# A spread of recurrence units, three operations on another engine, and seven early maps in a one-layer trunk kernel

## The chip, the cores and the metric

The kernel runs on one core of a Trainium2 chip. The metric is the device time of one execution in microseconds (us); lower is better. A core has TensorE (PE; its weight loads are shown apart as PEld), VectorE (DVE), ScalarE (ACT), GpSimd (POOL) and SyncE (SP), each with its own queue of instructions that it takes in order, and 16 DMA engines. Matrix results land in banks of PSUM, all else lies in SBUF or in DRAM.

## What is computed

The reference is one layer of a trunk for 512 latent tokens and 256 context tokens with a width of 1024. Cut to what matters here:

```python
p_l = modulate(x, norm1_g[l], mod[:, 0], mod[:, 1]) @ w_in[l]
pool_l, q_l, k_l, v_l, rw_l, gate_l = split_cols(p_l, IN_SPLITS)
att_l = diff_post(diff_attn_latent(qh_l, keys, vals, lam), subln_g[l], lam_init)
prep_c = rwkv_prepare(rw_c, *rw_par)
S_c, y_c = wkv_bidir(S0, *prep_c[:6])
prep_l = rwkv_prepare(rw_l, *rw_par)
_, y_l = wkv_bidir(S_c, *prep_l[:6])
rwo_l = rwkv_output(y_l, prep_l, r_k[l], gn_w[l], gn_b[l])
mix_l = merge_branches((pool_mixer(...), att_l, rwo_l), gate_l, w_br[l], w_out[l])
x = x + mod[:, 2] * mix_l
x = x + mod[:, 5] * hier_moe(f_l, *moe_par).reshape(B, L, D)
```

Three branches are merged: a pooling over windows of tokens, differential attention, and a recurrence that runs in both directions (`wkv_bidir`; each step updates a 64x64 state per head with a decay, a rank-one correction and a new key and value). A mixture of 32 experts follows.

## The kernel before

The recurrence is computed in chunks of 64 tokens. A unit is one of three groups of 256 tokens, one of two directions and one pair of heads (`g`, `d`, `hp`): 24 units. For each, `prep` makes the decays from a small matmul (L514, L515 into the banks `psm`): tanh on ScalarE (L518, L519), an affine step to a sigmoid (L520), a running sum `cum` (L522), exponentials of it (L524, L526) and, of the decays, the column `wc` at the end of each chunk (L527). From these come the scaled rows `abd`, `rbd` and `bk` (L531 to L540, of which L538 is an affine step on `ta`), and then products and transposes on TensorE (L552 to L584), masked by VectorE (L565, L587, L589) and copied by ScalarE (L571 to L591) into `ub`, which is stored in DRAM as `u_d`. After the eighth unit of a group `solve` loads small triangular blocks `pa_` of all eight from `u_d` and inverts them on VectorE, 30 steps of a product and an addition in sequence (L614, L616), and stores `t_d`.

`finish` makes of each unit its maps: it loads `tbd` from `t_d` and `ar` and `F` from `u_d`, and runs four steps of matmuls, L799, L805, L812 and then L831 (first group) or L824 (others), with copies on ScalarE between them (L800, L807), and additions on VectorE (L817, L833, L827). There are five `tbd` buffers. `steps` then runs the recurrence over the maps (L857).

The work is staged like this. First come the projections of the recurrence's inputs. Then the blocks for keys, queries and values (L231, token-major), pools and gates (L217, channel-major), each matmul three times with high and low parts of weights that ScalarE and GpSimd split (L211, L212); a pool block ends in a small matmul L684 into `psm`. A loop over these blocks starts one `prep` whenever enough steps have passed: `PACE = 34` spreads the 24 units over 34 of 52 steps. What is running lies in the list `active`, and each step of the loop (`tick`) advances each of its generators to its next `yield`. The last three gate blocks are `rest`. Then `NP = 4` turns of `finish` are begun before the pools of the first part are closed; the rest of the loop (`for i in range(NP, 24 + lag)`) begins a unit in each turn and advances attention by two pieces, and the recurrence by one step, once its maps are there. The scores of attention (L992, L993) go into one buffer `sc`; their softmax is L994 to L1004, the transposes are L1019, the weighted sums L1025, and the norm of a head ends in L1038. `bonus` makes a further term of the output (L904 to L919). The merges of the three branches (L1127), the output projection (L1418), the router and the experts (L1580, L1615, with weights loaded at L1231) follow.

The framework orders the instructions of each engine ahead of the run, by the order in which they are written and by priorities; `tc.high_priority(n)` moves what is written under it forward. Each engine's order is then fixed.

## Time and profile before

| | us |
|---|---|
| median of 3 runs | 1483.42 (1483.1 to 1486.53) |
| the profiled execution | 1484.0 |
| its span, first to last instruction | 1482.2 |
| PE busy | 1362.9 (92%) |
| DVE busy | 828.9 (56%) |
| ACT busy | 461.1 (31%) |
| POOL busy | 382.9 (26%) |

The shares are means over stages with different limits; what a stage waits for is read from stretches of the span. The mean granted clock of TensorE was 0.967. Idle time of an engine that does not set the pace costs nothing.

### The profile page before, as it was taken

Reading aid. Unit: us, or ns where it says so; the run is one execution under the profiler, and the core shown is the slowest. Engines: PE = TensorE matmul, PEld = TensorE weight load, DVE = VectorE, ACT = ScalarE, POOL = GpSimd, SP = SyncE. Lnnn points to the kernel's source line nnn. Section 1 sums busy time; section 2 is a strip of 40 time slices with the busy share of each in tenths; the row PEclk is TensorE's granted clock in tenths of the full one; section 3 lists DMA queues with packets and bytes.
Section 4 is the critical chain, followed back from the end, with each engine's and each line's share of the span. In section 5 each row is a group of like instructions: output and inputs, shape, how many; then the busy total and the mean of one; then the engine's idle time right before and its main releaser. Section 6 shows DMA issues by size and latency. Waiting matters only on the chain.

```text
span 1482.2 us, 23832 instructions
## 1 busy us (share of the span) xinstructions
PE 1362.9 (92%) x9076; PEld 1015.1 (68%) x9076; DVE 828.9 (56%) x1746; ACT 461.1 (31%) x1017; POOL 382.9 (26%) x345
## 2 busy tenths in 40 slices
PE   5999998898889898899999998995999999999987
PEld 3776787777779886788887776983555555445543
DVE  4553228789999765267777876452343343333324
ACT  4432244564545322234345423331110110111100
POOL 2111263354543343212221347110011111111101
PEclk9999999999899999799999999998999999999999
DMA  9368655565557673875747286479999999999996
GB/s 372 125 233 309 220 178 185 200 214 198 178 209 229 215 201 121 236 231 173 250 137 238 86 275 240 156 267 382 345 417 418 417 418 418 419 418 419 417 418 237
DMA packets 138615, 401.01 MB, mean 271 GB/s; under 512 B 38821, under 2 KB 69541, under 8 KB 107776
## 3 DMA queue, kind: packets, MB, share of 16 engines
q1 hardware_dynamic: 102640, 332.72, 61.0%
q10 hardware_dynamic: 32256, 58.47, 10.7%
q0 software_dynamic: 3600, 8.24, 1.7%
q8 instruction: 74, 1.21, 0.3%
q14 instruction: 45, 0.37, 0.1%
HBM read 344.47 MB, written 58.72 MB: 272 GB/s over the span
## 4 chain that ended last, share of the span: by engine, by line
PE 51%; DMA 27%; DVE 13%; issue 3%; ACT 2%; POOL 2%; SPq 1%; ACTq 0%; DVEq 0%; POOLq 0%
PE pp L217 11%; DMA ew<-in_w_eg_dram 8%; PE pp L1580 6%; DMA ew<-in_w_eu_dram 5%; DMA ew<-in_w_ed_dram 4%; PE pp L1127 4%; PE pp L1418 3%; PE pp L1615 3%; DVE ptmp L614 2%; PE pp L231 2%; PE pp L824 2%; PE sc L993 2%; PE pp L812 1%; PE pp L799 1%; PE pp L805 1%
## 5 line engine op out<-in xcount | busy, mean ns | idle before, releaser
L1580 PE MATMUL pp<-ew,xT 128*64 128x256 f32 x1888 | 225.4, 385 | 13.0 <-DMA ew<-in_w_eu_dram 7.1
L1580 PEld LDWEIGHTS pp<-ew,xT 128*64 128x64 f32 x1888 | 132.7, 137 | 93.5 <-issue 17.6
L217 PE MATMUL pp<-xll,wh 128*128 128x512 f32 x344 | 136.3, 397 | 0.9 <-DVE xll L317 0.7
L217 PE MATMUL pp<-xlh,wh 128*128 128x512 f32 x344 | 135.3, 404 | 1.3 <-DVE qn L666 1.0
L217 PE MATMUL pp<-xlh,wl 128*128 128x512 f32 x344 | 136.0, 396 | 0.0
L212 POOL TENSOR_TENSOR wl<-wraw,wh 128x512 fp32r<-128x512 f32 x84 | 115.1, 1399 | 75.4 <-ACT wh L211 71.7
L1633 POOL TENSOR_TENSOR yhl<-m,yhl 128x512 fp32r<-128x512 f32 x30 | 38.1, 1271 | 346.0 <-ACT yhl L1632 346.0
L1615 PE MATMUL pp<-ew,hT 128*64 128x512 f32 x440 | 101.4, 598 | 2.6 <-DMA ew<-in_w_ed_dram 2.6
L1586 DVE TENSOR_TENSOR hh<-hh,pp 128x256 f32<-128x256 f32 x32 | 13.5, 421 | 156.7 <-ACT hh L1585 156.7
L1618 DVE SCALAR_TENSOR_TENSOR m<-pp,gc,m 64x512 f32<-64x512 f32 x62 | 46.5, 750 | 85.1 <-PE pp L1615 73.3
L1625 DVE TENSOR_TENSOR x<-x,pp 128x512 f32<-128x512 f32 x128 | 79.8, 680 | 25.1 <-PE pp L1624 25.1
L211 ACT ACTIVATE wh<-wraw 128x512 fp32r<-128x512 f32 (+1 forms) x112 | 61.0, 614 | 61.8 <-PE pp L217 43.4
L217 PEld LDWEIGHTS pp<-xlh,wh 128*128 128x128 f32 x344 | 64.8, 190 | 19.3 <-issue 3.6
L217 PEld LDWEIGHTS pp<-xll,wh 128*128 128x128 f32 x344 | 65.2, 190 | 15.8 <-issue 1.8
L217 PEld LDWEIGHTS pp<-xlh,wl 128*128 128x128 f32 x344 | 65.2, 189 | 15.2 <-issue 1.1
L1615 PEld LDWEIGHTS pp<-ew,hT 128*64 128x64 f32 x440 | 29.4, 136 | 59.5 <-issue 48.2
L793 POOL TENSOR_TENSOR ao<-ar,cst 128x512 f32<-128x512 f32 x24 | 30.6, 1274 | 144.4 <-PE pp L805 81.8
L1594 ACT ACTIVATE hT<-psm 128x256 f32<-128x256 f32 x32 | 12.3, 384 | 157.4 <-PE psm L1592 129.7
L231 PE MATMUL pp<-wh,xlh 128*128 128x256 f32 x192 | 58.6, 305 | 0.0
L231 PE MATMUL pp<-wh,xll 128*128 128x256 f32 x192 | 56.8, 296 | 0.0
L231 PE MATMUL pp<-wl,xlh 128*128 128x256 f32 x192 | 56.6, 295 | 0.0
L1585 ACT ACTIVATE hh<-pp 128x256 f32<-128x256 f32 x32 | 12.3, 385 | 130.0 <-PE pp L1580 130.0
(407 smaller groups left out, 3112.0 us busy)
## 6 DMA issues: line engine op xcount, KB each, us to landing
ew<-in_w_eg_dram SPq DMA_DIRECT2D x59, 1024.0 KB
ew<-in_w_eu_dram SPq DMA_DIRECT2D x58, 1024.0 KB
ew<-in_w_ed_dram SPq DMA_DIRECT2D x56, 1024.0 KB
wraw<-in_w_in_dram SPq DMA_DIRECT2D x27, 1024.0 KB
u_d<-ub ACTq DMA_DIRECT2D x16, 1152.0 KB
wada<-in_w_adr_dram SPq DMA_DIRECT2D x16, 1024.0 KB
ar<-u_d SPq DMA_DIRECT2D x24, 640.0 KB
wa<-in_w_ad_dram SPq DMA_DIRECT2D x8, 1024.0 KB
```

What stands on the lines that cost most here:

```text
L211: S.activation(self.h[:, kk, :n], raw[:, kk, :n], AF.Copy)
L212: (eng[q % 2] if type(eng) is tuple else eng).tensor_sub(self.l[:, kk, :n], raw[:, kk, :n], self.h[:, kk, :n].bitcast(FT))
L217: PE.matmul(ps, a[:, k, cs], b[part][:, k], start=(k + n == 0), stop=(k == KD - 1 and n == 2))
L231: PE.matmul(ps, a[part][:, k, ts], b[:, k], start=(n == 0), stop=(n == 3 * KD - 1))
L793: G.tensor_mul(ao, aa[:, :, 2:3].to_broadcast([128, 4, 2, 64]), offm[:, None].to_broadcast([128, 4, 2, 64]))
L1127: PE.matmul(ps, a[:, k], bs[k][:, x], start=(c == 0), stop=(c == 11))
L1418: PE.matmul(p, a[:, ts], x[:, k], start=(k == 0 and c == 0), stop=(k == KD - 1 and c == 2))
L1580: PE.matmul(pg[64 * h:64 * h + 64, i], xT[:, k], of(w[i], k)[:, h * 256:h * 256 + 256], start=(k == 0), stop=(k == KD - 1), tile_position= ...
L1615: PE.matmul(pd[64 * h:64 * h + 64], hT[:, k], of(w[2], k)[:, h * 512:h * 512 + 512], start=(k == 0), stop=(k == 3), tile_position=(0, 64 * h))
L1618: V.scalar_tensor_tensor(y[ps_, h * 512:h * 512 + 512], pd[64 * h:64 * h + 64], gc, m5[ps_, h * 512:h * 512 + 512], op0=OP.mult, op1=OP.mult)
L1625: V.tensor_add(xt2[t][:, sl], xt2[t][:, sl], p)
L1633: eng.tensor_sub(yl, y[:, sl], yh.bitcast(FT))
```

## The change

`PACE` becomes 44, so the 24 units are spread over 44 of the 52 steps. Three operations per unit, L520, L527 and L538, become ACTIVATEs on ScalarE; the chunk ends `wc` are now exponentials of `cum` instead of copies of the decays. The blocks of `rest` are all written out before the first pools are closed, `NP` becomes 7, and the first seven turns of `finish`, and the memsets of their buffers, are written under a priority that moves them ahead, into the last projections. While these run, their matmuls use the two banks of `psm` instead of the six of `pp`, and the pools' last matmul L684 uses `pp` instead. The load of `pool_w` is written earlier into another pool, and `bonus` begins in a later turn.

```diff
--- before.py
+++ after.py
@@ -32,13 +32,13 @@
 GM = 6
 CL = 6
 AH = 5
-PACE = 34
+PACE = 44
 NF = 14
 NATT = 8
 PW = 4
 NG = 8
 NA = 4
-NP = 4
+NP = 7
 SW = 4
 FB = 2
 
@@ -346,6 +346,7 @@
     lpool = pa.enter_context(tc.tile_pool(name="lora", bufs=1, reuse_waits="tile"))
     wlT = lpool.tile([128, T], FT)
     alT = lpool.tile([128, T], FT)
+    pw = lpool.tile([128, 4, 128], FT)
 
     rw_ = pa.enter_context(ExitStack())
     rw = rw_.enter_context(tc.tile_pool(name="rwproj", bufs=1, reuse_waits="tile"))
@@ -517,14 +518,14 @@
         ta = wk.tile([128, 256], FT, name="ta", bufs=2)
         S.activation(sg, psw[:, 0:256], AF.Tanh, scale=0.5, bias=hb[:, dc:dc + 1])
         S.activation(ta, psw[:, 256:512], AF.Tanh, scale=0.5, bias=hb[:, 8 + dc:9 + dc])
-        V.tensor_scalar(sg, sg, 0.5, 0.5, op0=OP.mult, op1=OP.add)
+        S.activation(sg, sg, AF.Copy, scale=0.5, bias=0.5)
         cum = wk.tile([128, 256], FT, name="cum", bufs=1)
         V.tensor_tensor_scan(cum, K("scan"), sg, 0.0, OP.mult, OP.add)
         wt = wtb[u % NB]
         S.activation(wt[:, :, 1:65], c4(cum), AF.Exp, scale=DECAY)
         wi = wk.tile([128, 256], FT, name="wi", bufs=2)
         S.activation(wi, cum, AF.Exp, scale=-DECAY)
-        V.tensor_copy(wc[:, g, d, hp, :], wt[:, :, 64])
+        S.activation(wc[:, g, d, hp, :], c4(cum)[:, :, 63], AF.Exp, scale=DECAY)
         ab, rb = abd[u % NB], rbd[u % NB]
         for h in range(2):
             hs = slice(h * 64, h * 64 + 64)
@@ -535,7 +536,7 @@
         t1 = wk.tile([128, 256], FT, name="t1", bufs=1)
         V.scalar_tensor_tensor(t1, ta, 1.0, wi, op0=OP.add, op1=OP.mult)
         V.scalar_tensor_tensor(bk[:, :, 1], c4(t1), -0.5, c4(kk_), op0=OP.mult, op1=OP.mult)
-        V.tensor_scalar(ta, ta, ka[:, 0, hp:hp + 1], ka[:, 1, hp:hp + 1], op0=OP.mult, op1=OP.add)
+        S.activation(ta, ta, AF.Identity, scale=ka[:, 0, hp:hp + 1], bias=ka[:, 1, hp:hp + 1])
         V.tensor_mul(ta, ta, k_)
         V.tensor_mul(bk[:, :, 0], c4(ta), c4(wi))
         if lat:
@@ -619,14 +620,13 @@
         V.memset(pa_.rearrange("p i j -> p (i j)")[:, 0:1024:33], 1.0)
         nc.gpsimd.dma_start(t_d[g], pa_)
 
+    nc.sync.dma_start(pw, I["pool_w"])
 
     kp = pr_.enter_context(tc.tile_pool(name="qkv", bufs=1, reuse_waits="tile"))
     gq = kp.tile([128, 2, 64], FT)
     nc.sync.dma_start(gq, I["qkg"].partition_broadcast(128))
     tab = kp.tile([128, 4, 2, 64], FT)
     nc.sync.dma_start(tab, I["rope"])
-    pw = kp.tile([128, 4, 128], FT)
-    nc.sync.dma_start(pw, I["pool_w"])
 
     def qk_post(which, b, t, qn):
         yield 1
@@ -680,7 +680,7 @@
     def pool_post(g, u, cn):
         for _ in range(PW):
             yield 1
-        po = ps_sm()
+        po = ps_big()
         PE.matmul(po, pw[:, g], cn, start=True, stop=True)
         S.activation(u, po, AF.Copy, scale=P("ps", g))
         nc.scalar.dma_start(br_d[g], u)
@@ -728,6 +728,8 @@
             active.append(order.pop(0))
         next(rest, None)
         tick()
+    for _ in rest:
+        pass
     pr_.close()
     psol.close()
     dump("v_d", v_d)
@@ -758,12 +760,18 @@
     NT = 5
     tbd = [we.tile([128, 4, 128], FT, name=f"tbd{i}") for i in range(NT)]
     hbd = [we.tile([128, 4, 2, 2, 64], FT, name=f"hbd{i}") for i in range(2)]
-    for t_ in tbd + hbd:
-        V.memset(t_, 0.0)
+    with tc.high_priority(2000):
+        for t_ in tbd + hbd:
+            V.memset(t_, 0.0)
     units = {}
     cnt_f = [0]
 
+    early = [True]
+
     def ps2():
+
+        if early:
+            return ps_sm()
         return ppool.tile([128, 512], FT, name="pp", bufs=6)
 
     def finish(g, d, hp):
@@ -1068,11 +1076,10 @@
     lag = 6
     for i in range(NP):
         fin.append(finish(i // 8, i // 4 % 2, i % 4))
-        if i % 2:
-            next(rest, None)
-        turn(None, 0)
-    for _ in rest:
-        pass
+
+        with tc.high_priority(2000):
+            turn(None, 0)
+    early.clear()
     pa.close()
     psum = pb.enter_context(tc.tile_pool(name="psum2", space=PSUM, **TW))
     wk = pb.enter_context(tc.tile_pool(name="rwork", **TW))
@@ -1090,7 +1097,7 @@
             fin.append(finish(i // 8, i // 4 % 2, i % 4))
         g, j = divmod(i - 8 - lag, 8)
         turn(chains[g] if g >= 0 else None, 0 if i < NA else 2)
-        if 5 <= i < 13:
+        if NP < i < NP + 9:
             next(bon, None)
     wx.close()
     mgx = ctx.enter_context(ExitStack())
```

TensorE's order around the products of unit 24, before (line numbers are those of the file):

```order
L552 MATMUL psm<-cst,pr 128x2 x2
L563 MATMUL pp<-bk,abd_1700 128x128 x4
L569 MATMUL pp<-cst,bk 128x128 x4
L576 MATMUL pp<-cst,abd_1700 128x128 x4
L584 MATMUL pp<-rbd_1704,bk 128x128 x4
L231 MATMUL pp<-wh,xlh 128x256
L231 MATMUL pp<-wl,xlh 128x256
```

The same place after, where L553 to L585 are the lines L552 to L584 of before:

```order
L553 MATMUL psm<-cst,pr 128x2 x2
L564 MATMUL pp<-bk,abd_1701 128x128 x4
L570 MATMUL pp<-cst,bk 128x128 x4
L577 MATMUL pp<-cst,abd_1701 128x128 x4
L585 MATMUL pp<-rbd_1705,bk 128x128 x4
L217 MATMUL pp<-xlh,wh 128x512
L217 MATMUL pp<-xll,wh 128x512
```

Before, the last 120 matmuls of L231 (values) and 336 of L217 stand behind unit 24; after, no L231 and 216 of L217.

VectorE's order in the preparation of unit 24, before, where `pa__4521` and `ptmp` belong to the second `solve`:

```order
L520 TENSOR_SCALAR sg<-sg 128x256
L616 TENSOR_TENSOR pa__4521<-pa__4521,ptmp 128x30
L522 SCALAR_TENSOR_TENSOR cum<-cst,sg 128x256
L614 TENSOR_TENSOR ptmp<-pa__4521 128x29x2
L616 TENSOR_TENSOR pa__4521<-pa__4521,ptmp 128x29x2
L614 TENSOR_TENSOR ptmp<-pa__4521 128x28x3
L527 COPY wc<-wtb_1710 128x4
L531 TENSOR_TENSOR abd_1700<-lkk,wtb_1710 64x4x64 x2
```

And after, with lines that are one higher:

```order
L523 SCALAR_TENSOR_TENSOR cum<-cst,sg 128x256
L532 TENSOR_TENSOR abd_1701<-lkk,wtb_1711 64x4x64 x2
L537 SCALAR_TENSOR_TENSOR t_5088<-ta,wi 128x256
L538 SCALAR_TENSOR_TENSOR bk<-t_5088,lkk 128x4x64
L540 TENSOR_TENSOR ta<-ta,lk 128x256
L541 TENSOR_TENSOR bk<-ta,wi 128x4x64
```

The three operations are gone from VectorE's queue, and the second `solve` stands wholly ahead of this unit.

TensorE's order at the first maps, before, from the last projections to the first scores:

```order
L217 MATMUL pp<-xlh,wl 128x512
L799 MATMUL pp<-ar,tbd_5792 128x64 x4
L805 MATMUL pp<-z,ao 128x64 x4
L799 MATMUL pp<-ar,tbd_5793 128x64 x4
L812 MATMUL pp<-z_5844,tbd_5792 128x64 x4
L805 MATMUL pp<-z,ao 128x64 x4
L799 MATMUL pp<-ar,tbd_5794 128x64 x3
L992 MATMUL sc<-kh,qz 128x512
```

And after, where L807 is the first step of a map (L799 of before):

```order
L217 MATMUL pp<-xll,wh 128x512
L807 MATMUL psm<-ar,tbd_5792 128x64 x4
L217 MATMUL pp<-xlh,wl 128x512
L217 MATMUL pp<-xlh,wh 128x512
L217 MATMUL pp<-xll,wh 128x512
L217 MATMUL pp<-xlh,wl 128x512
L684 MATMUL pp<-wide,pw 128x512
```

The first map step now has 148 of the projections' matmuls behind it in TensorE's queue, and its result goes to a bank of `psm`; before, it stood behind the last projection. Up to the first score 6 groups of map matmuls stand before, and 21 after.

## Rows read from the trace of the kernel before

**Rows 1.** Stretches: length; busy time (instructions) of each engine; clock, DMA share, GB/s.
```profile
core 0: us, PE busy (x) PEld busy (x) DVE busy (x) ACT busy (x) POOL busy (x), PEclk, DMA share, GB/s
220.00:340.00 120.00, 107.92 (x713) 94.76 (x712) 98.21 (x242) 62.50 (x155) 51.48 (x49) 0.97 0.62 206
340.00:500.00 160.00, 139.48 (x881) 125.28 (x880) 154.03 (x356) 78.76 (x190) 66.60 (x63) 0.90 0.58 198
500.00:600.00 100.00, 93.05 (x443) 76.87 (x442) 53.48 (x107) 25.08 (x46) 38.13 (x32) 0.97 0.57 176
600.00:640.00 40.00, 34.19 (x180) 28.44 (x180) 15.79 (x35) 9.89 (x25) 9.16 (x12) 0.74 0.95 276
640.00:780.00 140.00, 140.00 (x1194) 121.15 (x1195) 97.01 (x185) 59.60 (x140) 32.60 (x34) 1.00 0.61 185
780.00:985.00 205.00, 193.44 (x1372) 164.05 (x1368) 144.56 (x310) 81.32 (x183) 70.55 (x54) 0.97 0.58 204
985.00:1482.00 497.00, 455.66 (x3093) 252.67 (x3092) 176.92 (x334) 66.20 (x132) 57.15 (x47) 0.98 0.97 393
```
**Rows 2.** Waits of SP's queue, 860 to 1000: total us, times, longest.
```profile
SPq L1231 <- PE pp L1418: 44.3, 4, 25.8
```
**Rows 3.** First unit's matmul (first and last start), unit 24's product and its mask.
```profile
L514 PE MATMUL psm<-wlT,w2p x48: 376/480/792, 218.5 to 462.7; 64*128 64x256 f32 x48
...
492.15 2.08 PE L563 MATMUL pp<-bk,abd 128*128 128x128 f32 x8 [5.27 <-DVE ub L565]
...
497.34 0.68 DVE L565 TENSOR_TENSOR ub<-pp,cst 128x512 f32<-128x512 f32 x1
```
**Rows 4.** Groups by line, DVE: count, busy us, mean ns, idle before.
```profile
L538 DVE TENSOR_SCALAR ta<-ta,ka 128x256 f32<-128x256 f32 x24 | 11.1, 461 | 0.0
L520 DVE TENSOR_SCALAR sg<-sg 128x256 f32<-128x256 f32 x24 | 8.2, 340 | 3.0 <-ACT sg L518 2.9
L527 DVE COPY wc<-wtb 128x4 f32<-128x4 f32 x24 | 6.2, 258 | 4.3 <-ACT wtb L524 4.3
```
**Rows 5.** Groups by line, ACT: three ACTIVATEs near to the new ones.
```profile
L519 ACT ACTIVATE ta<-psm,hb 128x256 f32<-128x256 f32 x24 | 11.3, 470 | 0.0
L526 ACT ACTIVATE wi<-cum 128x256 f32<-128x256 f32 x24 | 9.7, 402 | 0.0
L961 ACT ACTIVATE lm<-lm 128x2 f32<-128x2 f32 x1 | 0.2, 203 | 3.1 <-DVE lm L960 3.1
```
**Rows 6.** Chain of work that ended last: start, us, what; runs of projections, a pool matmul.
```profile
497.18 11.53 PE pp L231 x96
...
592.07 0.86 PE psm L684 x2
592.93 7.08 PE pp L217 x31
```
**Rows 7.** Timeline of PE: a unit's products and transposes at full clock.
```profile
241.50 1.05 PE L563 MATMUL pp<-bk,abd 128*128 128x128 f32 x8
242.39 0.60 PE L569 MATMUL pp<-cst,bk 128*128 128x128 f32 x4
```
**Rows 8.** Chain: the wait after the last projection, and the first score.
```profile
600.03 3.80 DMA lq<-in_lam_dram
...
609.32 0.53 PE sc L992
```
**Rows 9.** Chain: map steps at full clock, four matmuls each (eight records).
```profile
641.32 0.84 PE pp L799 x8
642.16 0.95 PE pp L831 x8
```
**Rows 10.** The third solve: its products on DVE, and SP's issue of its loads.
```profile
L614 DVE TENSOR_TENSOR ptmp<-pa__5148 x30: 183/357/1375, 532.2 to 563.6; 128x30 f32<-128x30 f32 x2, 128x58 f32<-128x58 f32 x2, 128x84 f32<-128x84 f32 x2, 128x108 f32<-128x108 f32 x2
...
516.81 8.10 SPq L609 DMA_DIRECT2D pa__5148<-u_d  x14
```
**Rows 11.** Timeline of PE: a score that waits for the softmax before it.
```profile
621.42 0.79 PE L992 MATMUL sc<-kh,qz 128*128 128x512 f32 x1 [2.32 <-ACT p L996]
```
**Rows 12.** Waits, 220 to 600: total us, times, longest.
```profile
ACT wtb L524 <- DVE cum L522: 30.3, 13, 6.2
```

## The prediction

> **What bounds the kernel now.** I read the stretches first, engine against engine [rows 1]. From 985 us on the weights of the experts set the pace: the DMA share is 0.97 over 497 us, and nothing of the change runs there. Where that stretch begins is set by TensorE: the loads of the expert weights wait in SP's queue 44.3 us for the matmuls of the output projection [rows 2]. So what the front gains moves the whole rest forward by as much.
>
> In the front the reader is to see two things. Between 340 and 500 us VectorE is busy 154.03 of 160 us, while TensorE has 139.48 and a granted clock of 0.90: TensorE waits for VectorE. Between 500 and 600 it is the reverse, VectorE 53.48 of 100 and TensorE 93.05. The preparation of the 24 units of the recurrence (`prep`) is packed into the first stretch, and plain projections are left for the second. Between 600 and 640 TensorE has only 34.19 of 40 at a clock of 0.74, then 140.00 of 140 at 1.00.
>
> How closely VectorE sets the pace: I added VectorE's instructions in their order from the first unit on, each with the mean duration of its group in the view by line. Up to the product mask L565 of unit 24 this gives 278.6 us. In the trace the first unit begins at 218.5 and this L565 at 497.34, a distance of 278.8 [rows 3]. So until then VectorE hardly ever rests, and every microsecond taken from it counts until another engine is the bound.
>
> **The change, part by part.**
>
> *Three operations to ScalarE.* VectorE loses L520, L527 and L538, 8.2 + 6.2 + 11.1 = 25.5 us [rows 4]. ScalarE gains three ACTIVATEs per unit. Nearest rows: 402 ns for one without a pointer operand (L526), 470 with one (L519), about 203 for a tiny one (L961) [rows 5]; 24 times 1.08 = 25.8 us. ScalarE is busy 78.76 of 160 us in the tight stretch [rows 1], so it has room, but its queue is in order (a rival, below). The new `sg` and `ta` follow the tanh on the same engine, which removes a crossing for `sg`.
>
> The rows say that the operations take about as long on either engine (340 and 461 ns against some 400 and 470), and that VectorE is the engine that is full. The Trainium skill, "ScalarE: Activation LUTs", section "Rules for kernel authors", speaks against the move: additions and multiplications belong on VectorE. By that rule the 25.5 us would stay on the engine that is full; this trace sides against it here, for that reason alone.
>
> *The spread.* Behind unit 24's products stand 120 matmuls of L231 and 336 of L217 before, and 216 of L217 after. So 120 and 120 move ahead of it. One takes 11.53/96 = 0.120 us and 7.08/31 = 0.228 us [rows 6]: 14.4 + 27.4 = 41.8 us of TensorE. At full clock TensorE's own sum up to there is 217 us before: 616 x 0.120 + 240 x 0.228 + 24 units of about 3.6 (0.89 us for L563, 0.44 for the transposes of L569 [rows 7], the rest alike) + 3 for the queries' and keys' transposes. After: 259. VectorE's sum after: 278.6 - 25.5, plus some 12 for the rest of the second `solve` and for pool additions that now come before: 265. So the bound passes from VectorE alone to both at once. Taking the larger of the two sums in stretches of four units, it is 279 before (the trace: 278.8) and 285 after; of three units 291 after, of each single unit 309. I take 293, since two engines that are both nearly full also wait for each other: unit 24 at +14 us. Bounds: 0 (TensorE never waits) and +30 (they trade places unit by unit).
>
> *From unit 24 to the first scores.* Before: 609.32 - 492.15 = 117.2 us [rows 3, 8]. After, in TensorE's order: rest of the unit 1.8; 216 x 0.228 = 49.2; four L684 at 0.86 = 3.4 [rows 6]; 14 groups of four map matmuls at 0.84 to 0.95 [rows 9], 12.6. Together 67. One wait is added: on VectorE the maps' additions (L817, L833) now stand between the steps of the third `solve`, and behind them are queued the fourth pool block's additions, which TensorE's L684 waits for. The last six loads of that `solve` stand in SP's queue behind the reload of the first map's `tbd`, which waits for that map's L812, 31 us after unit 24 by the same prices; with issue (16 loads took about 9 us) and landing the `solve` starts at about +42. Before it started at 532.2, +40 [rows 3, 10]. The second map's addition of L833 then comes some 5 us after TensorE wants it. I take 5 (0 to 13). 72 in all. From the last projection to the first score it is 600.03 to 609.32 [rows 8], 9.3 us, as the loads of attention wait for the memory of the projections in both. The `solve` itself takes 32 us [rows 10] and, with 5 us of other VectorE work in it, ends at about +79, just in time. 81, and 2 for maps at the lower clock: 83. So -34 (-39 to -26).
>
> *Seven maps early.* At the first score 21 groups of map matmuls are done instead of 6. 15 x 0.87 = 13 us leave the stretch from 640 on, where TensorE is busy without a gap [rows 1]. Two things are given back. The first three scores wait for each other (one buffer; 2.32 us idle before a score [rows 11]) and had three groups of maps between them as cover: 2.7 us. And the loop has three turns fewer, so that about three score steps of attention move behind it, among the merges; the last softmax then has no merge matmuls behind it to cover its chain and that of the head's norm. These are about 3.5 us (reduce, exp, weights) and 3.3 us (square, root, scale), 6.8 together. Net -3.5 (-10 if all is covered, +5 if the chains cost double). The later turns for `bonus` and the moved load of `pool_w` cost nothing: both are beside TensorE's matmuls. The other banks cost nothing where their two buffers are free: L514 and L552, which shared them, are done by then.
>
> *Sum:* +14 - 34 - 3.5 = -23.5. The profiled execution has a span of 1482.2 in 1484.0; the median of the runs, 1483.4, is 1.2 above the span. 1482.2 - 23.5 + 1.2 = 1460.
>
> **The rivals.**
>
> *No mutual waits.* Unit 24 moves by +3 only, all else as above: 1449. For it: ScalarE and GpSimd have room. Against: today TensorE is idle for 33 of 280 us between 220 and 500 [rows 1], not all of it VectorE's sums but queues as well. Chance 0.12.
>
> *They trade places unit by unit* (+30): 1476. For: the order alternates stretches with four projections and with two. Chance 0.10.
>
> *The third `solve` is late.* Its loads wait for a map, the map's loads wait behind a weight load on SP. If it starts 13 us later than reckoned, the pool blocks, the maps and the first scores, which stand behind it on VectorE, wait as long: 1473. Chance 0.10.
>
> *Slower: ScalarE's queue holds TensorE.* ScalarE takes its work in order. It waits 30.3 us in all for the running sum L522 [rows 12], with casts of weights (L211) queued behind, which TensorE needs. Today that is hidden, because TensorE has slack. If after the change it falls on TensorE in full, and the 25.8 us of added ACTIVATEs too, step one is +56 instead of +14: 1502. It decides from 42 us on, 1.75 us per unit. Against: ScalarE would be at about 57% of the stretch. The skill's rule named above would point this way. Chance 0.08.
>
> *It does not do what it says, or the gain is lost to the weights:* 1483. The order shows the maps among the last projections, and the weight loads wait for TensorE, not for a time. Chance 0.03.
>
> That leaves 0.57 for the forecast and its near surroundings.
>
> **How the numbers follow.** About 0.3% (4.5 us) is what a measurement of this kernel can tell from no change. Faster by more: the forecast, the first three rivals but for their upper edges: 0.85. Within 0.3%: 0.07, the upper edges and the last rival. Slower: 0.08. The predicted time is the forecast's, 1460. The bounds of the terms add to -49 and +9; they will not all fall on one side. From 1446 (below the case without waits) to 1480 (above the case that trades places) leaves out the slow rival and the last one, and a little below.
>
> **What would show it.** Right: VectorE no longer over 95% in any long stretch before 500; unit 24's L565 between 498 and 528; a last projection near 578 and a first score near 587; maps (L799 to L831) between projections; the experts' stretch unchanged in length and some 23 us earlier. Wrong: ScalarE's waits for `cum` followed by TensorE's waits for `wh` or `wl`; a wait of TensorE of more than 10 us at a map or at L684 for VectorE, ended by the `solve`; gaps of TensorE over 10 us in all at the end of attention.

## The result, and the profile after

The changed kernel takes 1494.49 us (median of five runs, 1491.13 to 1495.62), the kernel before 1486.53 beside it: a ratio of 1.0059, interval 1.0041 to 1.0077. It is slower by 0.6%; 23 us less had been predicted. The profiled executions have spans of 1493.9 and 1482.2 us, so 11.7 us are to be found.

Three places of TensorE's timeline after (start, duration, engine, line, what) cut the span into four: the products of unit 24, the first score, the first matmul of the output projection.

```profile
526.75 1.03 PE L564 MATMUL pp<-bk,abd 128*128 128x128 f32 x7
...
614.79 0.77 PE L1000 MATMUL sc<-kh,qz 128*128 128x512 f32 x1
...
923.47 0.28 PE L1425 MATMUL pp<-ew,ew 128*128 128x256 f32 x1
```

The same four stretches as windows, after (columns as in [rows 1]):

```profile
220.00:526.75 306.75, 280.85 (x1791) 248.19 (x1790) 249.53 (x544) 173.08 (x433) 134.17 (x126) 0.96 0.58 197
526.75:614.79 88.04, 79.83 (x418) 68.10 (x418) 51.27 (x108) 20.95 (x43) 32.08 (x32) 0.93 0.61 179
614.79:923.47 308.68, 279.28 (x1993) 225.91 (x1993) 212.22 (x367) 123.86 (x271) 90.20 (x77) 0.93 0.64 198
923.47:1493.90 570.43, 526.05 (x3671) 320.93 (x3669) 219.29 (x476) 90.73 (x194) 69.53 (x59) 0.98 0.91 369
```

and before, cut at the same instructions:

```profile
220.00:492.15 272.15, 239.55 (x1544) 212.20 (x1543) 244.76 (x579) 138.76 (x338) 118.08 (x111) 0.94 0.59 199
492.15:609.08 116.93, 107.78 (x534) 91.33 (x535) 63.18 (x133) 29.69 (x58) 44.05 (x42) 0.94 0.61 186
609.08:914.27 305.19, 291.13 (x2115) 238.46 (x2115) 213.14 (x379) 124.04 (x278) 93.99 (x81) 0.95 0.64 201
914.27:1482.20 567.93, 525.28 (x3671) 321.24 (x3669) 218.91 (x476) 90.86 (x194) 69.55 (x58) 0.98 0.92 372
```

Unit 24 comes 34.6 us later, the way from there to the first score is 28.9 shorter, the way from the first score to the output projection 3.5 longer, the rest 2.5 longer: 11.7 in all.

What the reader should do with such rows, and what the prediction did not do, is to split TensorE's time in each stretch in three. **Idle** is the length less the busy time. **Loss by the clock** is the time in which TensorE is busy, times one less the clock granted then (1.00 is 2.4 GHz, 0.50 is 1.2), added up from the trace; taken over the whole length it would count the idle time at the lower clock twice. What is left is the **work**, TensorE's time at full clock. From the first score to the output projection that is before 305.2 = 14.1 idle + 13.2 loss + 277.9 work, after 308.7 = 29.4 + 16.4 + 262.9. The 15 us of work that were taken out are there to be seen (x2115 to x1993 matmuls), and 18.5 us of idle and loss, most of it idle, have come in their place. The table in the next section has the split of every kernel. (The recorded expectations with such figures took the loss over the whole length: their idle and loss together is 1 to 7 us higher, and their work as much lower.)

Where the idle time came in, after. TensorE's waits from 614 to 923 (total us, times, longest):

```profile
PE sc L1000 <- ACT p L1004: 7.4, 3, 2.8
PE pp L807 <- ACT yt L926: 5.0, 1, 5.0
PE pp L1134 <- ACT mwh L1126: 4.8, 4, 2.3
PE pp L1027 <- DVE p L1012: 4.5, 2, 4.0
PE pp L1046 <- DVE o L1039: 4.4, 1, 4.4
```

and as windows, the first 40 us of attention and the 40 us around its last score:

```profile
614.79:634.79 20.00, 14.42 (x47) 9.50 (x46) 5.52 (x11) 4.50 (x10) 1.77 (x2) 0.55 1.05 283
634.79:654.79 20.00, 14.98 (x101) 13.26 (x100) 8.41 (x18) 5.03 (x14) 2.55 (x2) 0.83 1.00 308
...
834.79:854.79 20.00, 18.84 (x94) 14.40 (x92) 17.34 (x29) 8.82 (x21) 8.80 (x6) 1.00 0.42 124
854.79:874.79 20.00, 12.77 (x56) 11.26 (x57) 10.10 (x24) 5.32 (x11) 1.38 (x1) 0.74 0.47 150
```

In the first 40 us idle and loss are 18.4 us (10.8 before), in the 20 us from 854.79 on 11.1 (0.4 before, at the same distance from the first score). The last two waits of the list belong to that second place (4.0 us of the first of them): the last softmax and the last norm, with no merge behind them to cover them. The merges' waits for their weights (L1134) are not new: before had 6.2 us of them.

### The profile page after: what moved, and what is told of

It reads as the page before. It is cut to its first block, busy times and chain, and to the rows that moved or that the text cites. A ratio compares the mean times of both kernels' runs of the same rounds, so it can differ in the third digit from the quotient of the medians.

```text
span 1493.9 us, 23865 instructions
## 1 busy us (share of the span) xinstructions
PE 1363.7 (91%) x9076; PEld 1013.8 (68%) x9076; DVE 819.9 (55%) x1674; ACT 486.1 (33%) x1089; POOL 381.7 (26%) x345
## 3 DMA queue, kind: packets, MB, share of 16 engines
q10 hardware_dynamic: 32256, 58.47, 10.7%
## 5 line engine op out<-in xcount | busy, mean ns | idle before, releaser
L217 PE MATMUL pp<-xlh,wh 128*128 128x512 f32 x344 | 137.0, 409 | 3.3 <-ACT wide L410 1.7
L217 PE MATMUL pp<-xll,wh 128*128 128x512 f32 x344 | 136.0, 396 | 0.9 <-DVE xll L317 0.7
L217 PE MATMUL pp<-xlh,wl 128*128 128x512 f32 x344 | 136.1, 396 | 0.0
L1593 DVE TENSOR_TENSOR hh<-hh,pp 128x256 f32<-128x256 f32 x32 | 13.5, 421 | 158.6 <-ACT hh L1592 158.6
L217 PEld LDWEIGHTS pp<-xlh,wh 128*128 128x128 f32 x344 | 64.8, 190 | 22.8 <-issue 3.9
L211 ACT ACTIVATE wh<-wraw 128x512 fp32r<-128x512 f32 (+1 forms) x112 | 61.1, 614 | 47.0 <-PE pp L217 35.9
L217 PEld LDWEIGHTS pp<-xll,wh 128*128 128x128 f32 x344 | 65.4, 190 | 15.8 <-issue 1.8
L217 PEld LDWEIGHTS pp<-xlh,wl 128*128 128x128 f32 x344 | 65.3, 190 | 15.1 <-DVE wl L212 0.8
L1622 PEld LDWEIGHTS pp<-ew,hT 128*64 128x64 f32 x440 | 29.2, 136 | 60.1 <-issue 48.8
L1601 ACT ACTIVATE hT<-psm 128x256 f32<-128x256 f32 x32 | 12.3, 383 | 158.2 <-PE psm L1599 138.3
L231 PE MATMUL pp<-wh,xlh 128*128 128x256 f32 x192 | 57.9, 302 | 1.0 <-DVE ub L566 0.5
L231 PE MATMUL pp<-wh,xll 128*128 128x256 f32 x192 | 56.4, 294 | 0.0
L231 PE MATMUL pp<-wl,xlh 128*128 128x256 f32 x192 | 56.1, 292 | 0.0
L1592 ACT ACTIVATE hh<-pp 128x256 f32<-128x256 f32 x32 | 12.3, 384 | 132.8 <-PE pp L1587 132.8
```

The source lines that it names most:

```text
L211: S.activation(self.h[:, kk, :n], raw[:, kk, :n], AF.Copy)
L217: PE.matmul(ps, a[:, k, cs], b[part][:, k], start=(k + n == 0), stop=(k == KD - 1 and n == 2))
L231: PE.matmul(ps, a[part][:, k, ts], b[:, k], start=(n == 0), stop=(n == 3 * KD - 1))
L1622: PE.matmul(pd[64 * h:64 * h + 64], hT[:, k], of(w[2], k)[:, h * 512:h * 512 + 512], start=(k == 0), stop=(k == 3), tile_position=(0, 64 * h))
```

## The experiments

The loss was first looked for in the three parts of the change, each alone and in pairs; then the early maps and the operations were taken apart. One theory was that ScalarE's in-order queue gives VectorE's 25.5 us back as waits; the second, that the spread is the loss; the third, that the early maps are.

All kernels, from their profiled runs, in us; "to first score" starts at 220, "attention" runs from the first score to the first matmul of the output projection. Each pair is idle and loss by the clock together / work. Times are medians; the ratio is to the kernel before in the same runs.

| kernel | time | ratio, interval | first score | to first score | attention |
|---|---|---|---|---|---|
| before | 1482 to 1487 | | 609.1 | 61.6 / 327.4 | 27.3 / 277.9 |
| after (all three parts) | 1494.5 | 1.0041 to 1.0077 | 614.8 | 51.2 / 343.6 | 45.8 / 262.9 |
| e1 operations | 1463.7 | 0.9852 to 0.9887 | 582.1 | 35.5 / 326.7 | 28.0 / 279.1 |
| e2 pace 44 | 1475.7 | 0.9935 to 0.9978 | 595.6 | 47.2 / 328.4 | 26.5 / 278.1 |
| e3 early maps | 1500.7 | 1.0092 to 1.0128 | 624.1 | 62.8 / 341.3 | 48.8 / 261.8 |
| e4 operations, pace 44 | 1475.9 | 0.9932 to 0.9969 | 600.4 | 51.9 / 328.5 | 29.0 / 277.4 |
| e5 operations, early maps | 1485.9 | 1.0004 to 1.0042 | 608.1 | 46.4 / 341.8 | 42.1 / 263.2 |
| e11 early maps, four turns | 1493.9 | 1.0042 to 1.0097 | 615.1 | 63.3 / 331.8 | 33.7 / 275.4 |
| e12 seven turns, late | 1498.3 | 1.0088 to 1.0153 | 606.1 | 58.1 / 327.9 | 44.3 / 276.0 |
| e14 after, lag 9 | 1494.1 | 1.0056 to 1.0090 | 615.4 | 54.5 / 340.9 | 41.9 / 264.9 |
| e15 bonus later | 1483.3 | 0.9983 to 1.0011 | 607.4 | 60.4 / 327.0 | 25.6 / 278.2 |
| f6 maps 3 to 6 left out | 1489.7 | 1.0001 to 1.0051 | 606.0 | 59.3 / 326.7 | 48.6 / 263.9 |
| f1 a product of each map from the eighth on left out | 1477.4 | 0.9944 to 0.9976 | 608.3 | 61.0 / 327.3 | 35.8 / 262.9 |
| e17 `ta` only | 1480.8 | 0.9964 to 0.9998 | 606.6 | 56.3 / 330.2 | 26.3 / 278.7 |
| f3 `sg` and `wc` only | 1479.1 | 0.9948 to 0.9986 | 598.3 | 49.5 / 328.7 | 29.2 / 278.0 |
| e16 operations, pace 30 | 1471.4 | 0.9900 to 0.9940 | 594.4 | 44.8 / 329.7 | 29.1 / 279.1 |
| f7 operations, pace 36 | 1470.0 | 0.9882 to 0.9919 | 592.1 | 44.2 / 327.9 | 25.9 / 279.6 |
| e13 operations, pace 38 | 1477.9 | 0.9950 to 0.9991 | 599.3 | 53.3 / 326.0 | 31.7 / 279.5 |
| g1 operations, two turns | 1462.5 | 0.9843 to 0.9885 | 582.3 | 35.9 / 326.4 | 27.7 / 279.3 |
| g2 as g1, attention two turns earlier | 1470.7 | 0.9893 to 0.9934 | 583.2 | 37.5 / 325.7 | 36.6 / 278.8 |

### The three parts

**e1**, only the operations:

```diff
-        V.tensor_scalar(sg, sg, 0.5, 0.5, op0=OP.mult, op1=OP.add)
+        S.activation(sg, sg, AF.Copy, scale=0.5, bias=0.5)
-        V.tensor_copy(wc[:, g, d, hp, :], wt[:, :, 64])
+        S.activation(wc[:, g, d, hp, :], c4(cum)[:, :, 63], AF.Exp, scale=DECAY)
-        V.tensor_scalar(ta, ta, ka[:, 0, hp:hp + 1], ka[:, 1, hp:hp + 1], op0=OP.mult, op1=OP.add)
+        S.activation(ta, ta, AF.Identity, scale=ka[:, 0, hp:hp + 1], bias=ka[:, 1, hp:hp + 1])
```

> Of the change, only the three operations on ScalarE. Theory 1 (ScalarE's queue in order: the scan of VectorE waits for sg, and ScalarE waits for VectorE before it may overwrite ta): the 25.5 us taken from VectorE come back as waits; VectorE's wait for sg about 18 us in all and ScalarE's wait at ta about 27 us, and unit 24's products no more than 10 us earlier than the 492 of before; 1480 to 1495. Theory 2 (the loss is the spread of the units): without the spread VectorE's 25.5 us count almost in full, unit 24 at about 472 to 478, first score 8 to 15 us earlier, 1468 to 1476. Theory 3 (the loss is the early maps) says the same of this run as theory 2.

1463.7: the first theory falls, and the operations alone are a gain of 1.3%. Theories 2 and 3 had unit 24 right (475.18, for 472 to 478) but not the rest: the first score comes 27 us earlier, not 8 to 15, and the time lies below their range. Unit 24 is 17.0 us of that; the other 10 lie between it and the first score, where a wait of TensorE at a pool block is gone (first row below, from the waits of before, 492 to 609). The wait of ScalarE that the first theory named is there (waits of e1, 220 to 582: total us, times, longest), but it lies beside other work: TensorE's idle and loss to the first score fell from 61.6 to 35.5.

```profile
PE psm L684 <- DVE wide L708: 7.0, 1, 7.0
```
```profile
ACT ta L538 <- DVE t L536: 24.2, 16, 3.8
```

**e2**, only the spread (`PACE = 34` becomes 44):

> Of the change, only the units spread over more of the projections (the pace of 44 in place of 34). Theory 1: the spread alone leaves VectorE with its 278.6 us up to unit 24 and some 12 more, TensorE with 259; they wait for each other, unit 24 at +20 to +35; behind it the third solve takes its 40 + 32 us, so that the first score comes 0 to 10 us later than in before: 1483 to 1494. Theory 2: the spread is the loss, all of it: first score 6 to 15 us later, 1490 to 1500. Theory 3 (maps): the spread alone is a gain or nothing, 1475 to 1484.

1475.7, also a gain, though unit 24 comes at 524.58 (32 later, as the first theory said): the first score is 13.5 us earlier, not later, so the second theory falls as well, and only the third had the time.

**e3**, only the early maps (all other lines of the diff):

> Of the change, only the seven maps between the last projections, in the other banks, with the pool blocks drained before and three turns fewer later. Theory 3 (the maps are the loss): unit 24 stays near 492, the first score comes 5 to 10 us later, as 15 groups of maps (13 us of TensorE) are put before it and some of them wait for the additions in the solve; the stretch from there to the output projection is not shorter, since its tail lies open (TensorE waits 8 us more for softmax, norm and merge): 1490 to 1498. Theories 1 and 2: the maps are even, 1480 to 1487: what they add before the first score (up to 10) comes back after it.

1500.7: the maps are the loss, by more than the third theory said (1490 to 1498). Unit 24 stood at 492.14 and the first score came 15 us later (said: 5 to 10), by the 14 us of work put ahead of it; behind it attention has 16 us of work less and takes 5.4 us longer.

**e4**, operations and spread without the maps:

> The three operations on ScalarE and the spread together, without the early maps. Theories 1 and 2: unit 24 near 525, as with the whole change; the first score within 5 us of 609, and the whole at 1483 to 1492. Theory 3: all of the loss is gone and more, since the maps were it: 1470 to 1480.

1475.9, the third theory's time; the first score is at 600.4, and not within 5 us of 609. Beside the changed kernel (1494.5) this run has the price of the maps in place: with them the way from unit 24 to the first score takes 88.0 us instead of 71.1 (13.5 of it work), and attention is 2.3 longer instead of shorter. And the operations add nothing to the spread: 1475.7 without them. Why, is seen in the stretch up to unit 24 as windows, of e1, then e2, then e4:

```profile
220.00:475.18 255.18, 233.95 (x1547) 207.56 (x1546) 227.37 (x524) 161.60 (x410) 116.75 (x111) 0.96 0.63 212
```
```profile
220.00:524.58 304.58, 277.57 (x1781) 245.71 (x1781) 263.92 (x614) 149.40 (x360) 129.79 (x123) 0.96 0.59 199
```
```profile
220.00:529.24 309.24, 279.23 (x1784) 247.63 (x1783) 248.24 (x543) 172.81 (x432) 134.04 (x126) 0.96 0.58 197
```

At pace 44 VectorE is busy 263.9 of 304.6 us with its operations and 248.2 of 309.2 without them: it had 41 us free already, and taking more from it moved nothing. Before it was busy 244.8 of 272.2 there, TensorE's work was 225 us, and in e1 VectorE's busy time and unit 24 went back by the same 17 us.

**e5**, operations and maps at the old pace:

> The three operations on ScalarE and the early maps, with the units at the old pace of 34. The runs so far: the operations alone put the first score at 582.1 (609.1 in before), the early maps alone at 624.1, and the stretch from the first score to the output projection was 305 to 307 us without the early maps and 309 to 311 with them. Theory A (the early maps cost the same whatever stands before, since they are 13 us of TensorE's work put ahead of the first score that never come back behind it): first score 12 to 17 us later than with the operations alone, so 594 to 599, and 1476 to 1482 in all. Theory B (the cost is the meeting of the maps with the third solve, which is early here): first score within 8 us of 582, and 1466 to 1472.

1485.9, with the first score 26 us later than in e1 where theory A had 12 to 17: 15 of it are work, 11 are idle and loss. Theory B falls, A holds in its direction and is short in its size.

### Why the early maps give nothing back

**e11**, the early maps with `NP = 4`:

> The early maps alone, on the kernel before, but with four turns as before in place of seven. Theory A (turns: the three turns fewer take cover from attention, so that nothing comes back behind the first score): the first score comes 3 to 8 us later than in before, as some maps are early, and the stretch from there to the output projection is not longer than 305 us; 1483 to 1490. Theory C (the place: the maps among the last projections and the drained pool blocks cost, whatever their number): first score at 620 or later as with seven, 1495 or more.

1493.9, and neither theory is right: the first score is at 615.1, and attention takes 309.1. The way to the first score is 6.0 us longer (4.4 of it work, as 72 matmuls of maps stand ahead of it instead of 46), and attention 3.9, with 6.4 more of idle and loss. So the way in which the early maps are written costs some 10 us apart from the number of turns. Two waits of TensorE show where some of it lies (waits of e11, 220 to 615 and 615 to 924): one at a pool block, 7.0 us before, and one for loads of keys, none before. Which part does it, the priority, the two banks of `psm` or the pool blocks written out first, no run separates.

```profile
PE pp L684 <- ACT wide L410: 10.8, 1, 10.8
```
```profile
PE sc L1001 <- DMA kl<-k_d: 4.6, 1, 4.6
```

**e12**, the kernel before with `NP = 7` (and `NP < i < NP + 9` for bonus):

> The kernel before with seven turns in place of four ahead of attention's loop, but all of them where the four stood, after the projections, in their own banks (the steps of bonus come as late as in the changed kernel). Theory A (turns): the stretch from the first score to the output projection does not get shorter by the 13 us of maps that it no longer holds, or TensorE idles 10 us more there; 1488 to 1500. Theory C (place): the 13 us come back, 1480 to 1487.

1498.3, with attention at 320.3 us: theory A's time, though not for its reason. The edit did not move the maps: 48 of their matmuls stand ahead of the first score (46 before) and 720 in attention (722 before), so the stretch still holds them, and the run tells what three turns less cost with the same work. The waits of the tail are there (waits of e12, 606 to 926), but idle grew by 4.7 us only; 12.3 are loss by the clock, most of it in the first 40 us (windows):

```profile
PE pp L1019 <- DVE p L1004: 5.2, 3, 4.0
PE pp L1038 <- DVE o L1031: 3.9, 1, 3.9
```
```profile
606.05:626.05 20.00, 19.36 (x89) 17.11 (x88) 5.88 (x11) 3.07 (x8) 2.96 (x3) 0.59 1.05 332
626.05:646.05 20.00, 20.00 (x90) 17.74 (x90) 7.04 (x15) 4.01 (x10) 2.53 (x2) 0.56 0.81 220
...
613.00:642.00 29.00, 29.00 (x120) 26.00 (x120) 9.34 (x19) 5.93 (x14) 3.81 (x3) 0.50 0.95 303
```

**e14**, the whole change with `lag = 9`, which gives attention its three turns back:

> The whole change, with attention's loop three turns longer at its end (the lag of the recurrence's steps 9 in place of 6), so that the score steps get back the turns that the seven early ones took. TensorE's time from the first score to the output projection splits into idle, loss by the lower clock, and the rest; the rest was 276 us in before and 257 in the changed kernel, idle and loss together 30 and 52. Theory A (turns): the waits at the end of attention (weights transposed 4.0, norm 4.4, merges 4.8) fall under 1 us each, idle and loss fall to 35 to 42, and the stretch is 290 to 300 instead of 308.7; 1476 to 1487. Rival (work taken ahead of the first score is simply missing as filler at the beginning and in the middle, turns or not): the stretch stays at 304 to 312, 1489 to 1497.

1494.1. The tail was covered again (L1027 0.7 us, L1046 0.3; 0.4 us of idle and loss in its 20 us instead of 11.1), the merges' waits stayed at 6.2, and the time did not move: TensorE waits 11.5 us for the softmax before a score instead of 7.4, and attention is 306.8 us instead of 308.7. Theory A falls as the explanation; the rival's numbers came.

**e15**, bonus three turns later, nothing else (`5 <= i < 13` becomes `8 <= i < 16`):

> The kernel before with the eight steps of bonus three turns later and nothing else. It tells apart what the seven turns cost (all kernels with seven turns had bonus three turns later as well). Theory A (turns): nothing, within 4 us of 1483, and the stretch from the first score to the output projection at 303 to 308. Rival (bonus): most of the 15 us that the kernel with seven late turns lost, the stretch at 315 to 321 and 1493 to 1500.

1483.3: bonus by itself costs nothing.

**f1** and **f6** take work out without putting it anywhere. f1 leaves out the second of the four products from the eighth map on, f6 all products of the third to sixth map:

```diff
+        pzv = z[:, :, 0:w]
+        if i < 7:
             pz = ps2()
```
```diff
+        skip = 2 <= i < 6
+        if not skip:
+            for c in range(4):
+                PE.matmul(pxv[:, c], tb[:, c], rr[:, c, 0:w], start=True, stop=True)
...
```

> The kernel before with one of the four products of each map (L805, some 1 us of TensorE) left out from the eighth map on: about 17 us of TensorE's work taken evenly out of the stretch from the first score to the output projection. Its length is 305 us in before, of it 276 work, 14 idle, 15 loss by the clock. Theory D (the stretch is TensorE's own work where the filler lies evenly): 286 to 292. Rival E (the stretch has another bound, a chain of attention or of the steps, near 305 whatever TensorE has to do; the early maps gave nothing back because of it): 300 to 306.

> The kernel before with the TensorE products of the third to sixth map left out (their copies and additions run on the data at hand): some 14 us of TensorE's work taken out of the beginning of attention, with nothing put ahead of the first score and the turns as before. This is the part of the early maps that should have been the gain. Theory D with place (at the beginning the maps are the filler while the first scores wait for each other; without them idle and loss of the clock rise there): the stretch gets shorter by 3 to 8 us only, idle and loss in its first 40 us from 12 to 17 to 22. If the work counts whole: 290 to 293 in place of 305. Rival E: 303 to 306.

f1: 15.0 us less work, attention 6.5 us shorter. f6: 14.0 us less work, attention 7.3 us **longer**. Neither came out at a theory's number: f1 lies between D and E, f6 is worse than all of them. But together they say where it goes. The first 60 us of attention as windows, before and then f6:

```profile
609.08:629.08 20.00, 16.39 (x65) 12.87 (x65) 6.57 (x14) 4.78 (x11) 1.97 (x2) 0.59 1.00 282
629.08:649.08 20.00, 20.00 (x145) 17.30 (x145) 11.81 (x26) 7.72 (x21) 3.82 (x3) 0.99 0.82 267
649.08:669.08 20.00, 20.00 (x144) 16.97 (x143) 12.76 (x26) 7.29 (x17) 3.26 (x3) 1.00 0.70 207
```
```profile
606.00:626.00 20.00, 13.65 (x43) 9.70 (x43) 8.44 (x16) 5.56 (x13) 6.65 (x6) 0.50 1.06 304
626.00:646.00 20.00, 13.86 (x58) 10.62 (x57) 10.33 (x21) 5.51 (x14) 0.00 (x0) 0.67 1.00 315
646.00:666.00 20.00, 18.81 (x71) 14.53 (x70) 8.43 (x16) 6.23 (x15) 2.54 (x2) 0.59 0.26 75
```

Before, TensorE stands idle 3.6 us there and has the higher clock from 629 on. Without the four maps it idles 13.7 us and its clock is 0.50, 0.67 and 0.59 for the whole 60 us: idle and loss by the clock are 33.6 us instead of 10.8. TensorE's waits for the softmax before a score grew from 5.9 us in attention to 14.0; a score that waited 2.32 us [rows 11] waits 6.14 in f6:

```profile
637.92 0.80 PE L1005 MATMUL sc<-kh,qz 128*128 128x512 f32 x1 [6.14 <-ACT p L1009]
```

This is the gain that the early maps were to bring, measured by itself: no gain, and in the profiled execution 7 us lost. How large the loss is in the time is less sure, since the executions of f6 lie between 1478.6 and 1495.9 us and the ratio's interval begins at 1.0001.

### Which operation, and which pace

**e17**, only `ta` on ScalarE, and **f3**, only the other two:

> The kernel before with only the operation on ta moved to ScalarE: 11.1 us less on VectorE, of the 25.5. Theory 1 (each microsecond of VectorE counts while VectorE is full, whatever ScalarE does): first score 9 to 13 us earlier, 1470 to 1475. Rival (the gain of the three is that of the scan's and the exponentials' chain, sg and wc, while ta only adds a wait of ScalarE for VectorE): within 4 us of 1483.

> The kernel before with the operations on sg and wc moved to ScalarE and ta left on VectorE (14.4 us of the 25.5). ta alone gave nothing (first score 606.6). If sg and wc carry the gain of the three: first score 580 to 588, 1460 to 1468. If the three only gain together (VectorE has to fall below TensorE's own time before TensorE stops waiting): first score 594 to 603, 1471 to 1480.

`ta` moves the first score by 2.5 us, the other two by 10.8, all three by 27. Rival and second case hold: the operations gain together, more than the sum of the parts. In e17 VectorE's 11.1 us are gone from L538, yet it is as busy as before up to 493 us. Other groups of the same count became longer, first before, then e17 (by line; count, busy us, mean ns):

```profile
L537 DVE SCALAR_TENSOR_TENSOR bk<-t,lkk 128x256 f32<-128x256 f32 x24 | 11.1, 461 | 0.1
...
L539 DVE TENSOR_TENSOR ta<-ta,lk 128x256 f32<-128x256 f32 x24 | 10.1, 421 | 0.2
```
```profile
L537 DVE SCALAR_TENSOR_TENSOR bk<-t,lkk 128x256 f32<-128x256 f32 x24 | 13.4, 560 | 0.1
...
L539 DVE TENSOR_TENSOR ta<-ta,lk 128x256 f32<-128x256 f32 x24 | 11.8, 494 | 0.2 <-ACT ta L538 0.2
...
L527 DVE COPY wc<-wtb 128x4 f32<-128x4 f32 x24 | 10.3, 431 | 5.1 <-ACT wtb L524 5.1
```

L527 was 258 ns [rows 4]. These three groups took 8.1 of the 11.1 us back, and four more steps of the second `solve` lie before 493; a few groups became shorter, the most by 2.5 us. But it is not that each instruction takes longer. The shortest, the median and the longest one (ns) show it, before and then e17:

```profile
L527 DVE COPY wc<-wtb x24: 155/164/718, 223.3 to 468.8; 128x4 f32<-128x4 f32 x24
```
```profile
L527 DVE COPY wc<-wtb x24: 153/170/4324, 225.3 to 470.5; 128x4 f32<-128x4 f32 x24
```

The medians of L537 and L539 stand likewise, at 416 and 415 ns before and 419 and 416 in e17. A few instructions are held long, and each of the eleven in e17 that took over 0.55 us lies over work of GpSimd. The longest, on VectorE, ends with the casts that GpSimd runs beside it:

```profile
430.13 4.32 DVE L527 COPY wc<-wtb 128x4 f32<-128x4 f32 x1 [0.57 <-ACT wtb L524]
```
```profile
430.68 3.74 POOL L212 TENSOR_TENSOR wl<-wraw,wh 128x512 fp32r<-128x512 f32 x3
```

So part of what looks like VectorE's work is time beside GpSimd. ScalarE's queue does stand at `ta` (waits of e17, 220 to 493), but VectorE waits for its result only 0.2 us in all (L539 above):

```profile
ACT ta L538 <- DVE t L536: 40.2, 20, 5.2
```

**e16, f7, e13**: the operations at paces of 30, 36 and 38.

> The three operations on ScalarE with a closer pace, 30 in place of 34, without the early maps. Theory A (with less work on VectorE the pace can go back, TensorE keeps more plain projections to cover the third solve): unit 24 at 462 to 470, idle and loss of clock up to the first score not over 39 us, 1458 to 1466. Rival (the pace of 34 is the balance, closer VectorE is full again): more idle of TensorE before unit 24, first score at 586 to 595, 1468 to 1477.

> The three operations on ScalarE at a pace of 36, without the early maps: beside 34 (1463.7), 30 (1471.4), 38 (1477.9) and 44 (1475.9). If idle and loss of the clock up to the first score go up with the pace (38.9 us at 34, 58.1 at 38): 1468 to 1474. If 38 was an unlucky order: 1461 to 1467.

> The three operations on ScalarE with a pace of 38, between 34 (1463.7) and 44 (1475.9), without the early maps. Theory A (past 34 the spread only puts the third solve later, which takes some 60 us from the last unit to its end and then holds the first score): the first score 4 to 8 us later than 582, 1466 to 1471. Theory B (a spread a little wider fits the lighter VectorE better): 1456 to 1463.

1471.4, 1470.0, 1477.9: all are slower than 34 with 1463.7. For e16 the rival held, for f7 the growing loss; for e13 neither. Its third solve ended at 557.6 and was not what the first score waited for. What grows on both sides of 34 is idle and loss to the first score: 44.8 (30), 35.5 (34), 44.2 (36), 53.3 (38), 51.9 (44), with the work equal within 4 us.

### A version that beats both

e1 beats both kernels. **g1** goes against the change with fewer turns ahead of attention (`NP = 2`), **g2** also begins attention earlier (`NA = 2`):

> The three operations on ScalarE and only two turns of maps ahead of attention's loop in place of four, attention itself beginning at the same turn as before: the other way from the change, more filler for the beginning of attention. What is reached with the operations alone is 1463.7, first score 582.1, with 12 us of idle and loss of the clock in the first 40 us behind it. If filler at the beginning is what counts: those 12 to 17 us fall, 1455 to 1462. If four turns are enough: 1461 to 1467. If the maps between the last projection and the first score, which fill the wait for attention's loads, are lost: first score 585 to 592, 1465 to 1473.

> As the run before, but attention begins two turns earlier as well, so that its loop has two turns more. If turns and filler both count: idle at the end of the stretch not over 8 us, 1455 to 1462. If the stretch has all the turns that it can use: within 4 us of the run before.

g1 is e1 again (1462.5; the first score at 582.3, and nearly the same waits). It does not tell whether four turns are enough, since the same 32 matmuls of maps stand ahead of the first score in both. g2 loses 8 us. In its profiled execution attention is 8.5 us longer than in g1, and its first 20 us are 9.8 us idle at a clock of 0.50; TensorE waits there for loads of keys, 3.8 and 5.1 us (the longer wait, from the waits of g2, 583 to 898):

```profile
PE sc L993 <- DMA kl<-k_d: 5.1, 1, 5.1
```

The best found is the three operations alone, at 0.987 of the time before; g1 is not to be told from it.

## Why the prediction was wrong, step by step

**What bounds the kernel** was read rightly in the main: VectorE to unit 24, TensorE from there. But that VectorE "hardly ever rests" does not follow from the sum of 278.6 us. Its recorded instructions overlap: from the first unit to the L565 of unit 24 their durations add to 283 us, while its busy time there is 250.9 of 278.8 us (window before):

```profile
218.50:497.34 278.84, 246.24 (x1577) 218.41 (x1577) 250.88 (x592) 140.56 (x343) 119.58 (x112) 0.93 0.60 200
```

That the sum met the distance was luck. In e1 unit 24 came 17.0 us earlier, not the 25.5 of the removed instructions, and VectorE's busy time up to it fell by 17.4.

**The three operations** failed where they met the spread. The step gave them 25.5 us off VectorE's sum and let the spread put 12 on; the bound passed to both engines. VectorE is busy 249.5 of 306.8 us, so its sum is indeed no longer the bound. But such a sum buys nothing, and e2 beside e4 shows that it bought nothing. The rival that ScalarE's queue holds TensorE falls with e1, and after the change TensorE waits for ScalarE only 2.2 us before unit 24, though the rival's time, 1502, was the nearest on the side that came true. On the rule of the Trainium skill ("ScalarE: Activation LUTs", section "Rules for kernel authors") that additions and multiplications belong on VectorE: e1 sides against it here by 20 us, e17 shows one such operation that gained next to nothing.

**The spread** is the first mis-sized term: +14 predicted (0 to +30), 34.6 measured. The working put TensorE's sum up to unit 24 at 217 us before and 259 after, "at full clock". The work is 225.0 and 268.9, so its growth of 42 was right (43.9). What failed is the time beside the work, TensorE's waits and its lower clock. By the step's own figures it falls from 62 us (279 less 217) to 34 (293 less 259). Measured, it fell only from 47.1 to 37.8, of which 25.9 are idle; e1, the best kernel, has 29.3. To land at +14, 17 would have had to do. The waits are the mutual ones that the step named and priced too low: 23.6 us of the idle time still end at VectorE. The largest (waits after, 220 to 526.75):

```profile
PE psm L515 <- DVE ql L641: 6.2, 3, 4.1
PE psm L637 <- DVE coef L556: 3.5, 2, 2.7
PE psm L553 <- DVE ql L641: 3.0, 1, 3.0
```

The rival with units trading places (+30) came nearest.

**From unit 24 to the first score** 83 was predicted and 88.0 measured. The order of events was right: the third `solve` starts 48 us after unit 24 (predicted 42) and ends at 83 (79), and TensorE's wait for it is 6.3 us (5). The row of that wait does not resolve the releaser, but the addition of a map that stands among the steps of the `solve` on VectorE ends at 583.00, and the matmul starts at 583.11:

```profile
582.15 0.85 DVE L825 TENSOR_TENSOR hbd<-psm,z 64x256 f32<-64x256 f32 x2
```
```profile
583.11 0.66 PE L807 MATMUL psm<-ar,tbd 128*128 128x64 f32 x2 [6.28 <-issue]
```

What the step did not ask is how the way looks without the maps: in e4 the third `solve` starts 24 us after unit 24 and the way takes 71.1. Whether six banks in place of the two of `psm` would have hidden the wait, no run shows.

**Seven maps early** is the second mis-sized term and the one with the wrong sign: -3.5 predicted (-10 to +5), +3.5 measured, and the 13 us of maps ahead of the first score were already in the 83. The work that left is 15 us. The two things given back were named in the prediction, the first scores' cover and the last softmax and norm, at 2.7 and 6.8 us. They measure 7.6 (first 40 us) and 10.7 (the tail). With the waits came a lower clock (0.55, 0.83 and 0.74 in the windows), and in the first 40 us a place not foreseen: ScalarE's queue stands 10.4 us at a store of bonus, until by the profile a load of attention has landed, while the share of the DMA engines is 1.00, and the map L807 waits 5.0 us for that (ScalarE's waits after, 614.79 to 680). The data of the store had been there since 641.2, and it was issued at 648.8; why it waited for that load, no run shows.

```profile
ACT yt L926 <- DMA qz<-q_d: 13.2, 2, 10.4
```

What failed is the premise that 13 us of work less are 13 us where TensorE is busy without a gap; f6 refutes it directly. Of the prediction's signs of being wrong the last one came near: 8.4 us of waits for the last softmax and norm at the end of attention, where it had said over 10.

**The experts' stretch** was to keep its length. It is 2.5 us longer; it lies between 567.8 and 573.2 in all the kernels here, and no run shows why it differs.

**The range** (1446 to 1480) and the chance for slower, 0.08, missed because the two mis-sized terms lie on one side: 20.6 us of the 35.2 are the spread's, 7.0 the maps', 5.1 the way's to the first score and 2.5 the experts'. Both of the first two took too little for TensorE's idle time and lower clock. What stays open: which part of the early maps' writing costs e11 its 10 us; why the parts' losses in e12 and f6 do not add up in the whole change (17 and 21 in idle and loss, 18.5 in the changed kernel); and why 34 is the best pace.

## What to carry to other kernels

Split the busiest engine's stretch into idle, loss by the clock and work before adding terms: a forecast that leaves the work as it is can only gain from the other two, and here 35.5 us of them, up to the first score, was the least that any kernel reached. Work that looks like load can be cover: before moving it ahead, leave it out where it stands and see whether that makes the stretch shorter at all. And time a change's parts one by one: here one part was worth 20 us, one 8, both together 8, and the third cost 17 by itself and 22 on top of the best.

## What the runs showed of the hardware

In e12 TensorE has matmuls without a gap from 613 to 642 us, most of them 64 to 128 columns wide, and the granted clock stays at 0.50 (1.2 GHz) through all of it (last row of the windows of e12); before, it was at 0.99 from 20 us behind the first score. What raised it there and not here, no run shows.

The mean duration of a group of VectorE's instructions can change though the instructions do not: in e17 L527 went from 258 to 431 ns with its median at 170 (164 before), and one instruction of 4.32 us beside casts of GpSimd, where 0.17 is the rule, makes up the whole difference. All instructions over 0.55 us of L527, L537 and L539, before and in e17, lie over GpSimd's work; no run took that work away, so that it is the cause is not shown by an experiment. So the sum of the durations removed is not what the engine gains: in e17 most of it came back, and in e1, with 25.5 us of them removed, VectorE's busy time up to unit 24 fell by 17.
